# Handing a normalisation its tokens channel by row, with its squares summed by short matmuls

## The chip, the cores and the metric

The kernel runs on one core of a Trainium2 chip. The metric is the time of one execution on the device in microseconds, as a median over runs. A profiled execution gives, beside its own time, a trace of every engine: PE (TensorE, the matmuls), PEld (TensorE's weight loads), DVE (VectorE), ACT (ScalarE), POOL (GpSimd) and SP (SyncE, whose queue issues most transfers).

## The reference

Two layers over 256 latent tokens `x` and 256 context tokens `ctx`, each 2048 channels wide. The first layer normalises both, modulates them with a scale and a shift from a conditioning vector, and projects them with one wide matrix. Neighbourhood attention and a bidirectional state-space scan follow, an output projection and a residual; the second layer is a gated short convolution. What bears on the change is this:

```python
def rms_norm(x, g):
    xf = x.astype(jnp.float32)
    y = xf * lax.rsqrt(jnp.mean(xf * xf, axis=-1, keepdims=True) + EPS)
    return (y * g.astype(jnp.float32)).astype(x.dtype)
...
shift, scale, gate = adaln(c, ada_w[i], ada_b[i])
h = modulate(rms_norm(x, norm_g[i]), shift[:, None], scale[:, None])
...
shift_c, scale_c, gate_c = adaln(c_ctx, ada_w[i], ada_b[i])
hc = modulate(rms_norm(ctx, norm_g[i]), shift_c, scale_c)
...
p = h @ w_in
pc = hc @ w_in[:, base:]
```

So h = x * r * A + S, where r is one factor for a token (the norm), and A and S are one value for a channel, A = (1 + scale) * norm_g and S = shift, with a pair of A and S for x and another for ctx.

## The kernel before

**Channel blocks and segments.** The 2048 channels are the contraction of the first projection. They stand on the partitions in 16 blocks of 128 (`kb`), and the kernel takes them two by two in eight segments (`j`): for each segment the modulation values are made (`ada_gen`), then h for its two blocks, then the products with the segment's rows of the first K, V, Q and B columns are added to open sums. The columns of `hH` and `hL` are 512 tokens, numbered in four tiles t of 128: 0 and 1 are x, 2 and 3 are ctx.

**Split numbers.** A value is held as a high part rounded to fp32r and a low part, the difference. Each product is three matmuls: hH with the weight's high part, hL with the high part, hH with the low part. `hH` is written by ScalarE (L757), `hf`, the same in full fp32, by VectorE (L759), `hL` by VectorE as their difference (L763). A weight's high part is a cast on ScalarE (`split`, L420), its low part a subtraction on VectorE (`low_part`, L427). The very first weight (K of segment 0) is split in two halves (`split_half`, L440 and L443).

**The normalisation.** `x_load` brings a tile of 128 tokens, a token on each partition. `x_norm` squares and sums it in four pieces of 512 channels, ScalarE (L601) and VectorE (L603) in turn, sums the four (L607), makes the factor r with `rstd` (VectorE L571, then a power on POOL, L572), and multiplies the tile by r (L613, L615). `x_pair` then turns two channel blocks at a time with TensorE transposes of 128x128 (`turn`, L199), 64 in all, and copies them out of PSUM (L628 on ScalarE, L629 on VectorE) to `xnT`, channel on the partition. `x_gen` runs this for x, and for each tile of ctx alone in segment 0.

**The modulation.** For each segment and each of scale and shift, four quarters of 512 KB (`in_ada`) are multiplied with the conditioning vectors (`cpad`): four matmuls 128x256 to a quarter, on four groups of 32 columns. ScalarE copies the sum (`half`, L724), two transposes turn it, VectorE adds up the groups (L732) and adds the constants (L735 to L738).

**The order.** The program is written out once, at build, by a planner: `urgent`, `side` and `back` hold generators, each of which yields the engine and the operands that its next instruction needs; `pump` runs those whose operands are ready by the planner's own clock, and `force` runs on until a condition holds. Each engine then runs its instructions in that order and waits in order. Loads go out from a list (`loads`) in order as buffers come free; all are on SP's queue: the eight quarters of segment 0, its K, V and Q weights (512 KB each), ctx, the second parts of two small constant arrays (`small`, `const`), B's weight, segment 1's eight quarters, and so on. The matmul loop of segment 0 does K, V and Q for the tiles of x, then waits for tile 2 of ctx, does K and V for it, then tile 3, then B. In later segments K goes over all four tiles, then V, then Q (x only), then B. `part_gen` moves each K and V sum to SBUF (L787 copies, L789 adds).

## Time and profile before

| | |
|---|---|
| time, median of 3 runs | 1761.66 us (1761.09 to 1764.66) |
| profiled execution: its own time | 1760.31 us |
| profiled execution: span in the trace | 1758.5 us |
| PE busy | 1736.7 us (99%) |
| PEld busy | 1463.1 us (83%) |
| DVE busy | 1223.6 us (70%) |
| ACT busy | 773.4 us (44%) |
| POOL busy | 31.6 us (2%) |
| HBM traffic over the span | 215 GB/s |

Busy time is the time in which an engine has an instruction under way; the shares are of the span. The own time holds the span and 1.8 us around it. In the groups of the profile a row gives a line, an engine, an operation, output<-input by the program's names, shapes and count, then busy us and the mean ns of one, then the idle time just before and what ended it. A timeline row gives the start, the length, and the same description, with the idle time before it in brackets. The recorded matmuls of one fp32 product are two where those of an fp32r product are one.

### The profile page before, as it was taken

The page shows a single profiled execution, that of the slowest core. Times are in us where ns is not written, and L with a number is a line of the kernel's source. Part 1 is how long each engine was busy: PE and PEld are TensorE (multiplying, and loading weights), DVE is VectorE, ACT ScalarE, POOL GpSimd, SP SyncE. Part 2 cuts the span into 40 slices and gives each one's busy share as a digit, 9 for nine tenths or more (in the row PEclk, how much of TensorE's full clock was granted, in tenths as well). Part 3 has the DMA queues.
Part 4 walks back from the last instruction along what each step waited for, and adds up shares of the span by engine and source line. Part 5 has one row for each costly group of instructions (what it writes and reads, how often), then busy time and mean ns, then how long its engine had stood idle before and what let it go on. Part 6 is the DMA issues. An engine that isn't in the chain of part 4 may idle for free.

```text
span 1758.5 us, 25025 instructions
## 1 busy us (share of the span) xinstructions
PE 1736.7 (99%) x9451; PEld 1463.1 (83%) x9451; DVE 1223.6 (70%) x1978; ACT 773.4 (44%) x1330; POOL 31.6 (2%) x28
## 2 busy tenths in 40 slices
PE   6999999999999999999999999999999999999998
PEld 4777988889888889888888898888888888888887
DVE  5666887878685878686877787787668555555554
ACT  5333544445242436343435343564446444444442
POOL 0000100001000000000000000000000000000000
PEclk9999999999999999999999999999999999999999
DMA  9987644686756767656776557768767666666563
GB/s 362 342 307 258 209 143 138 183 246 191 234 165 195 219 205 227 210 175 210 220 213 193 166 185 255 246 221 284 274 222 228 195 188 192 192 191 188 190 208 121
DMA packets 202536, 377.66 MB, mean 215 GB/s; under 512 B 32384, under 2 KB 69040, under 8 KB 202416
## 3 DMA queue, kind: packets, MB, share of 16 engines
q1 hardware_dynamic: 195152, 369.49, 65.5%
q10 hardware_dynamic: 7264, 6.58, 1.1%
q8 instruction: 74, 1.21, 0.3%
q14 instruction: 46, 0.38, 0.1%
HBM read 370.62 MB, written 6.71 MB: 215 GB/s over the span
## 4 chain that ended last, share of the span: by engine, by line
PE 94%; DMA 2%; DVE 2%; issue 1%; ACT 0%; POOL 0%; SPq 0%; ACTq 0%; DVEq 0%; POOLq 0%
PE bank L195 91%; PE bank L199 3%; DMA tmp<-dram_csr 1%; DVE w L427 1%; DMA raw<-in_ada 0%; DMA tmp<-dram_exr 0%; DMA raw<-in_adaT 0%; DVE tmp L1235 0%; ACT w L420 0%; POOL statk L572 0%; DVE mix L1562 0%; SPq L583 0%; DVE raw L823 0%; DVE tmp L603 0%; DVE Vt L1012 0%
## 5 line engine op out<-in xcount | busy, mean ns | idle before, releaser
L420 ACT CAST w<-raw 128x1024 fp32r<-128x1024 f32 x343 | 359.5, 1049 | 530.4 <-PE bank L195 447.7
L427 DVE TENSOR_TENSOR w<-raw,w 128x1024 fp32r<-128x1024 f32 x343 | 416.6, 1217 | 231.4 <-ACT w L420 230.1
L195 PE MATMUL bank<-hH,w 128*128 128x256 f32 (+1 forms) x2064 | 488.0, 324 | 1.2 <-DVE w L427 1.1
L195 PE MATMUL bank<-w,hH 128*128 128x512 f32 x1280 | 407.4, 396 | 2.7 <-ACT hH L757 2.5
L195 PEld LDWEIGHTS bank<-hH,w 128*128 128x128 f32 x2064 | 344.7, 188 | 34.2 <-DVE w L427 2.1
L195 PE MATMUL bank<-hL,w 128*128 128x256 f32 (+1 forms) x1040 | 334.3, 321 | 0.0
L195 PEld LDWEIGHTS bank<-w,hH 128*128 128x128 f32 x1280 | 237.7, 189 | 54.4 <-issue 4.0
L195 PE MATMUL bank<-w,hL 128*128 128x512 f32 x640 | 249.9, 391 | 0.1
L195 PEld LDWEIGHTS bank<-hL,w 128*128 128x128 f32 x1040 | 196.3, 189 | 14.9
L195 PE MATMUL bank<-w,h 128*128 128x512 f32 x768 | 179.7, 390 | 0.0
L823 DVE CUSTOM_DVE_ANT_0 raw<-raw,csb 128x1024 f32<-128x1024 f32 x128 | 155.4, 1219 | 26.2 <-DMA raw<-in_adaT 24.0
L195 PEld LDWEIGHTS bank<-w,h 128*128 128x128 f32 x768 | 143.6, 188 | 29.6
L195 PEld LDWEIGHTS bank<-w,hL 128*128 128x128 f32 x640 | 120.5, 188 | 25.4 <-DVE hL L763 0.6
L195 PE MATMUL bank<-w,mix 128*128 128x512 f32 x588 | 138.3, 391 | 0.9 <-DVE w L427 0.9
L195 PEld LDWEIGHTS bank<-w,mix 128*128 128x128 f32 x588 | 109.5, 188 | 24.0 <-DVE w L427 1.3
L1235 DVE SCALAR_TENSOR_TENSOR tmp<-bank,cwh,tmp 128x508 f32<-128x508 f32 (+1 forms) x96 | 71.0, 744 | 1.8
L195 PE MATMUL bank<-KL,h 128*128 128x512 f32 x264 | 63.8, 389 | 0.0
L427 DVE TENSOR_TENSOR KL<-raw,KL 128x1024 fp32r<-128x1024 f32 x32 | 39.1, 1223 | 33.1 <-ACT KL L420 33.1
L427 DVE TENSOR_TENSOR wL<-raw,wH 128x1024 fp32r<-128x1024 f32 x31 | 37.9, 1224 | 33.5 <-ACT wH L420 33.4
L427 DVE TENSOR_TENSOR QL<-raw,QT 128x1024 fp32r<-128x1024 f32 x32 | 39.2, 1224 | 29.8 <-ACT QT L420 29.8
L195 PEld LDWEIGHTS bank<-KL,h 128*128 128x128 f32 x264 | 49.5, 188 | 10.2
L195 PE MATMUL bank<-QT,h 128*128 128x512 f32 x168 | 56.2, 391 | 0.0
(291 smaller groups left out, 1984.7 us busy)
## 6 DMA issues: line engine op xcount, KB each, us to landing
raw<-in_w_in SPq DMA_DIRECT2D x196, 512.0 KB, 3.9
raw<-in_adaT SPq DMA_DIRECT2D x128, 512.0 KB, 4.8
raw<-in_sc_in SPq DMA_DIRECT2D x128, 512.0 KB, 3.8
raw<-in_w_out SPq DMA_DIRECT2D x64, 512.0 KB, 5.0
raw<-in_ada SPq DMA_DIRECT2D x34, 512.0 KB, 6.9
raw<-in_sc_out SPq DMA_DIRECT2D x32, 512.0 KB, 4.1
PT<-in_ada SPq DMA_DIRECT2D x16, 512.0 KB, 6.9
raw<-in_w SPq DMA_DIRECT2D x16, 512.0 KB, 6.1
```

The costliest lines, as they stand in the source:

```text
L195: E(T.matmul(o, l, r, start=start, stop=stop, skip_group_check=True))
L199: E(T.transpose(o, i, ident if k == 128 else ident[:k, :k]))
L420: E(S.copy(H, v))
L427: E(V.tensor_tensor(out=Lo, in0=v, in1=H.bitcast(F32), op=ALU.subtract))
L823: E(V.tensor_tensor_reduce(out=raw, in0=raw, in1=csb, scale=1.0, scalar=0.0, op0=ALU.mult, op1=ALU.add, accum_out=gp[:, h, m:m + 1]))
L1235: E(V.scalar_tensor_tensor(out=do, in0=di, scalar=cwh[:, 32 * k + ch:32 * k + ch + 1], in1=do, op0=ALU.mult, op1=ALU.add))
```

## The change

The tokens come with the channels already on the partitions: beside `x`, which stays for the residual, the kernel gets `xt`, and in place of `cx` it gets `ct`, both turned by the host before the launch. The 64 transposes, their copies, the scaling of the tiles and `x_norm`, `x_pair` and `x_gen` go.

- `squares(c)` (c = 0 for x, 1 for ctx): eight squares 128x512 on ScalarE, each of two channel blocks for 256 tokens; six adds on VectorE bring the first seven into one; the sum over the partitions is by matmuls of 128x1 with a column of ones, four on the accumulated squares and four on the last, 16 in all for x and ctx. VectorE and POOL make r for 128 tokens by 2; two transposes of r, broadcast along a row, give r as a row on all partitions, and ScalarE copies it to `Rb`.
- In `ada_gen` hf is now x * A * Rb on VectorE, hH = hf + S on ScalarE behind it, and hL = (hf + S) - hH on VectorE, in 256 wide pieces for x and ctx (before, hL was one 512 wide from segment 1 on). The quarters of segment 0 are multiplied one by one as they come, no longer two by two.
- `c_load` brings all of ctx in six transfers (two of 512 KB, four of 256 KB) behind K and V of segment 0 and ahead of Q. Two pieces lie in the places of `QT` and `QL`, four in those of later hL blocks. The second parts of `small` and `const` come after the weights of segment 3.

```diff
 
     xrow = [st([128, D], "KT", name="x0")]
-    QT, Vt, gt = st([128, 4, 256], "QT", F32R), st([128, 4, 512], "Vt"), st([128, 4, 256], "gt")
+    cplace = [st([128, 1024], "QT", name="c0")]
+    Vt, gt = st([128, 4, 512], "Vt"), st([128, 4, 256], "gt")
     xrow.append(st([128, D], "KL", name="x1"))
-    QL = st([128, 4, 256], "QL", F32R)
+    cplace.append(st([128, 1024], "QL", name="c1"))
     sz, xtm, yi = st([128, 4, 256], "sz"), st([128, 2, 512], "xtm"), st([128, 4, 256], "yi")
     PT = [st([128, 4, 256], f"PT{k}") for k in range(2)]
 
@@ -527,11 +528,9 @@
             weight(w0, 3 * j + (CK, CV, CQ).index(c), 2, 0, 512)
 
     q_ada(0)
-    w_seg(0, CK, CV, CQ)
-    loads.append(lambda: x_load(2))
-    loads.append(lambda: x_load(3))
-    loads.append(lambda: E(DMA.dma_start(sm[:, NFIRST:], small[:, NFIRST:])))
-    loads.append(lambda: E(DMA.dma_start(cs_[:, CFIRST:], const[:, CFIRST:])))
+    w_seg(0, CK, CV)
+    loads.append(lambda: c_load())
+    w_seg(0, CQ)
     weight(w_in, 0, 2, COL_B, 256)
     q_ada(1)
     for j in range(1, 8):
@@ -540,6 +539,9 @@
             q_ada(j + 1)
         w_seg(j, CQ)
         weight(w_in, j * 256, 2, COL_B, 256)
+        if j == 3:
+            loads.append(lambda: E(DMA.dma_start(sm[:, NFIRST:], small[:, NFIRST:])))
+            loads.append(lambda: E(DMA.dma_start(cs_[:, CFIRST:], const[:, CFIRST:])))
     loads.append(later_loads)
...
-    XS = {}
     ssq = st([128, 16], "ssq")
-
-    def x_load(t):
-        src = x if t < 2 else cx
-        r0 = (t % 2) * 128
-        xt = xrow[t] if t < 2 else st([128, D], ("KT", "KL")[t % 2], name=f"x{t}")
-        for q in range(0, 4, 2):
-            E(DMA.dma_start(xt[:, q * 512:(q + 2) * 512], src[r0:r0 + 128, q * 512:(q + 2) * 512]))
-            XS[4 * t + q], XS[4 * t + q + 1] = (xt[:, p * 512:(p + 1) * 512] for p in (q, q + 1))
-
-    x_load(0)
-    x_load(1)
+    for k in range(2):
+        for h in range(2):
+            hs = slice(h * 1024, (h + 1) * 1024)
+            E(DMA.dma_start(xrow[k][:, hs], xt[k, :, hs]))
...
-    xnT = [st([128, 512], ("Bl", "Cl")[kb] if kb < 2 else f"hL{kb}", name=f"xm{kb}") for kb in range(KB)]
+    one, Rb, *lplace = [st([128, 512], ("Bl", "Cl")[kb] if kb < 2 else f"hL{kb}", name=f"p{kb}") for kb in range(KB)]
+    E(V.memset(one, 1.0))
+    cplace += lplace[10:]
+    xT = [[xrow[k // 8][:, (k % 8) * 256:(k % 8) * 256 + 256], None] for k in range(KB)]
     rx = st([128, 4], "rx")
 
-    def x_norm(t):
-        yield when(lambda: 4 * t + 3 in XS and (t < 2 or ("h", 0, 0) in got))
-        for q in range(4):
-            xt = XS[4 * t + q]
-            yield W_("ACT" if q % 2 == 0 else "DVE", xt)
-            jk = tmp()
-            if q % 2 == 0:
-                E(S.activation(jk, xt, AF.Square, accum_out=ssq[:, 4 * t + q:4 * t + q + 1]))
-            else:
-                E(V.tensor_tensor_reduce(out=jk, in0=xt, in1=xt, scale=1.0, scalar=0.0, op0=ALU.mult, op1=ALU.add,
-                                         accum_out=ssq[:, 4 * t + q:4 * t + q + 1]))
-            give(free_t, jk)
-        yield W_("DVE", ssq[:, 4 * t:4 * t + 4])
-        E(V.tensor_reduce(out=rx[:, t:t + 1], in_=ssq[:, 4 * t:4 * t + 4], axis=AX.X, op=ALU.add))
-        rstd(rx[:, t:t + 1], rx[:, t:t + 1], D, EPS, 1)
-        for q in range(4):
-            xt = XS[4 * t + q]
-            yield W_("DVE" if q % 2 else "ACT", rx[:, t:t + 1])
-            if q % 2 == 0:
-                E(S.mul(xt, xt, rx[:, t:t + 1]))
-            else:
-                E(V.tensor_scalar(out=xt, in0=xt, scalar1=rx[:, t:t + 1], scalar2=None, op0=ALU.mult))
-
-    def x_pair(k2, ts):
-
-        yield W_("PE", *[XS[4 * t + k2 // 2] for t in ts], nb=1)
-        ps = bank()
-        n = 128 * len(ts)
-        for k in range(2):
-            kb = 2 * k2 + k
-            for i, t in enumerate(ts):
-                turn(ps[:, k * n + i * 128:k * n + (i + 1) * 128], XS[4 * t + kb // 4][:, (kb % 4) * 128:(kb % 4) * 128 + 128])
+    def c_load():
+        n = 0
+        for p in cplace:
+            m = p.shape[1] // 256
+            E(DMA.dma_start(p, ct[:, n * 256:(n + m) * 256]))
+            for k in range(m):
+                xT[n + k][1] = p[:, k * 256:(k + 1) * 256]
+            n += m
+
+    def squares(c):
+
+        yield when(lambda: xT[15][c] is not None)
+        acc, ps = None, None
+        for k in range(0, KB, 2):
+            src = xrow[k // 8][:, (k % 8) * 256:(k % 8) * 256 + 512]
+            if c:
+                src = cplace[k // 4][:, (k % 4) * 256:(k % 4) * 256 + 512] if k < 8 else cplace[k // 2 - 2]
+            yield W_("ACT", src)
+            sq = tmp()
+            E(S.activation(sq, src, AF.Square))
+            if k < KB - 2:
+                if k == 0:
+                    acc = sq
+                    continue
+                yield W_("DVE", sq)
+                E(V.tensor_tensor(out=acc, in0=acc, in1=sq, op=ALU.add))
+                give(free_t, sq)
+                continue
+            for p in (acc, sq):
+                yield W_("PE", p, nb=0 if ps is not None else 1)
+                f = ps is None
+                if f:
+                    ps = bank()
+                for h in range(2):
+                    for t in range(2):
+                        mm(ps[:, t:t + 1], p[:, h * 256 + t * 128:h * 256 + (t + 1) * 128], one[:, :1], f and not (h or t), True)
+                give(free_t, p)
+        r = rx[:, 2 * c:2 * c + 2]
+        yield W_("DVE", ps)
+        E(V.tensor_scalar(out=r, in0=ps[:, :2], scalar1=1.0 / D, scalar2=EPS, op0=ALU.mult, op1=ALU.add))
+        E(G.tensor_tensor(out=r, in0=r, in1=mhalf[:, :2], op=ALU.pow))
+        yield W_("PE", r)
+        for t in range(2):
+            turn(ps[:, 256 + t * 128:256 + (t + 1) * 128], r[:, t:t + 1].to_broadcast([128, 128]))
         yield W_("ACT", ps)
-        o = slice(ts[0] * 128, ts[0] * 128 + n)
-        E(S.copy(xnT[2 * k2][:, o], ps[:, 0:n]))
-        E(V.tensor_copy(xnT[2 * k2 + 1][:, o], ps[:, n:2 * n]))
+        E(S.copy(Rb[:, c * 256:(c + 1) * 256], ps[:, 256:]))
         give(free_b, ps)
-        got.update(("xm", t, k2) for t in ts)
-
-    def x_gen(c):
-
-        ts = (2 * c, 2 * c + 1)
-        for t in ts:
-            yield from x_norm(t)
-            if c:
-                yield from x_pair(0, (t,))
-        for k2 in range(c, KB // 2):
-            yield from x_pair(k2, ts)
+        got.add(("r", c))
...
-                    w_ = 2 if j == 0 else 4
...
-            for ts in ((0, 1), (2,), (3,)) if j == 0 else ((0, 1, 2, 3),):
...
+            for cs in ((0,), (1,)) if j == 0 else ((0, 1),):
+                yield when(lambda: all(("r", c) in got for c in cs))
+                o = slice(256 * cs[0], 256 * cs[-1] + 256)
                 for kb in (2 * j, 2 * j + 1):
...
-                    yield W_("DVE", xnT[kb][:, o])
+                    yield W_("DVE", Rb[:, o])
                     hf = tmp()
                     if hH[kb] is None:
                         hH[kb] = st([128, 512], f"hH{kb}", F32R, name=f"hH{kb}")
-                    if ts == (0, 1):
+                    if cs == (0,):
                         split_half(kb)
-                    for k, ok_ in spans:
-                        E(S.activation(hH[kb][:, ok_], xnT[kb][:, ok_], AF.Identity, scale=A0[:, kb, k:k + 1],
-                                       bias=S0[:, kb, k:k + 1]))
-                        E(V.tensor_scalar(out=hf[:, ok_], in0=xnT[kb][:, ok_], scalar1=A0[:, kb, k:k + 1],
-                                          scalar2=S0[:, kb, k:k + 1], op0=ALU.mult, op1=ALU.add))
+                    for c in cs:
+                        oc = slice(256 * c, 256 * c + 256)
+                        E(V.scalar_tensor_tensor(out=hf[:, oc], in0=xT[kb][c], scalar=A0[:, kb, c:c + 1], in1=Rb[:, oc],
+                                                 op0=ALU.mult, op1=ALU.mult))
+                        E(S.activation(hH[kb][:, oc], hf[:, oc], AF.Identity, scale=1.0, bias=S0[:, kb, c:c + 1]))
                     if hL[kb] is None:
                         hL[kb] = st([128, 512], f"hL{kb}", F32R, name=f"hL{kb}")
-                    E(V.tensor_tensor(out=hL[kb][:, o], in0=hf[:, o], in1=hH[kb][:, o].bitcast(F32), op=ALU.subtract))
+                    for c in cs:
+                        oc = slice(256 * c, 256 * c + 256)
+                        E(V.scalar_tensor_tensor(out=hL[kb][:, oc], in0=hf[:, oc], scalar=S0[:, kb, c:c + 1],
+                                                 in1=hH[kb][:, oc].bitcast(F32), op0=ALU.add, op1=ALU.subtract))
                     give(free_t, hf)
-                    if ts == (0, 1):
+                    if cs == (0,):
                         halfsplit.pop()()
-                if ts == (0, 1):
+                if cs == (0,):
                     hold[0] = False
                     split()
                     split()
-                got.update(("h", j, t) for t in ts)
+                got.update(("h", j, t) for c in cs for t in (2 * c, 2 * c + 1))
...
-    spawn(urgent, x_gen(0), 1)
+    spawn(urgent, squares(0), 2)
     spawn(urgent, ada_gen(), 2, 1)
-    spawn(urgent, x_gen(1), 1)
+    spawn(urgent, squares(1), 2)
...
+    QT, QL = st([128, 4, 256], "QT", F32R), st([128, 4, 256], "QL", F32R)
...
-        'x': f('x')[0], 'cx': f('ctx')[0], 'ada0': ada0, 'w0': w0, 'adaT': adaT, 'w_in': f('na_ssd_w_in')[0],
+        'x': f('x')[0],
+        'xt': f('x')[0].T.reshape(2, 8, 128, 256).transpose(0, 2, 1, 3).reshape(2, 128, 2048),
+        'ct': f('ctx')[0].T.reshape(16, 128, 256).transpose(1, 0, 2).reshape(128, 4096),
+        'ada0': ada0, 'w0': w0, 'adaT': adaT, 'w_in': f('na_ssd_w_in')[0],
```

More of the change, by code (lines that the diff above doesn't have):

```diff
@@ L141, with kernel @@
 @with_exitstack
-def kernel(ctx: ExitStack, tc, x, cx, ada0, w0, adaT, w_in, w_out, sc_in, sc_out, rpb, small, const,
+def kernel(ctx: ExitStack, tc, x, xt, ct, ada0, w0, adaT, w_in, w_out, sc_in, sc_out, rpb, small, const,
                        strict, rows, out):
@@ L709, in ada_gen @@
                     key = ("ada", j, part, q)
-                    w_ = 2 if j == 0 else 4
+                    w_ = 1 if j == 0 else 4
                     if q % w_ == 0:
@@ L739, in ada_gen @@
                 give(free_b, ps)
-            for ts in ((0, 1), (2,), (3,)) if j == 0 else ((0, 1, 2, 3),):
-                yield when(lambda: all(("xm", t, j) in got for t in ts))
-                spans = [(k, slice(max(256 * k, 128 * ts[0]), min(256 * k + 256, 128 * ts[-1] + 128)))
-                         for k in range(2) if {2 * k, 2 * k + 1} & set(ts)]
-                o = slice(128 * ts[0], 128 * ts[-1] + 128)
+            for cs in ((0,), (1,)) if j == 0 else ((0, 1),):
+                yield when(lambda: all(("r", c) in got for c in cs))
+                o = slice(256 * cs[0], 256 * cs[-1] + 256)
                 for kb in (2 * j, 2 * j + 1):
@@ L1989 @@
     force(lambda: not urgent, (urgent,))
-_INS = ['x', 'cx', 'ada0', 'w0', 'adaT', 'w_in', 'w_out', 'sc_in', 'sc_out', 'rpb', 'small', 'const', 'strict', 'rows']
+_INS = ['x', 'xt', 'ct', 'ada0', 'w0', 'adaT', 'w_in', 'w_out', 'sc_in', 'sc_out', 'rpb', 'small', 'const', 'strict', 'rows']
 def kernel(**inputs):
```

## The prediction

> **What bounds the kernel now.** I read first the page's chain of work that ended last, then the busy time by stretches, then PE's timeline up to 56 us, then ScalarE's and VectorE's there.
>
> ```profile
> PE 94%; DMA 2%; DVE 2%; issue 1%; ACT 0%; POOL 0%; SPq 0%; ACTq 0%; DVEq 0%; POOLq 0%
> ...
> 21.00:24.50 3.50, 1.89 (x12) 0.96 (x8) 1.92 (x6) 2.70 (x6) 0.00 (x0) 1.00 1.03 406
> 24.50:28.00 3.50, 3.50 (x10) 2.73 (x10) 3.40 (x6) 3.08 (x7) 0.00 (x0) 0.52 1.02 405
> 28.00:33.50 5.50, 5.50 (x26) 4.50 (x25) 2.68 (x10) 3.32 (x6) 0.55 (x1) 0.99 1.05 399
> 33.50:45.00 11.50, 9.75 (x99) 6.19 (x98) 6.69 (x23) 6.90 (x19) 1.06 (x3) 1.00 0.84 326
> 55.00:165.00 110.00, 109.78 (x747) 80.62 (x746) 65.49 (x124) 34.28 (x54) 0.00 (x0) 1.00 0.84 305
> ```
>
> The columns of the stretches are the stretch, its length, busy PE, PEld, DVE, ACT, POOL, then the granted TensorE clock, the DMA share and GB/s. From 55 to 165 us PE rests 0.22 us in all, and the chain is 94% PE: once the first projections run, whatever PE has lost stays lost to the end. VectorE is busy 65 of 110 us there, ScalarE 34, so small work added or removed on them is hidden. The change's instructions all lie ahead of that, so its worth is the moment at which PE reaches the common work, the first group of the second segment.
>
> ```profile
> 10.82 2.28 PE L195 MATMUL bank<-raw,cpad 128*32 128x256 f32 x16 [10.82 <-DMA raw<-in_ada]
> 13.03 4.36 PE L199 MATMUL bank<-const,x 128*128 128x128 f32 x32
> 23.35 0.74 PE L195 MATMUL bank<-w,hH 128*128 128x512 f32 x2 [1.11 <-ACT hH L757]
> 33.40 0.38 PE L199 MATMUL bank<-const,x 128*128 128x128 f32 x2
> 35.13 0.50 PE L195 MATMUL bank<-w,hH 128*128 128x512 f32 x1 [1.36 <-ACT hH L757]
> 38.82 0.87 PE L199 MATMUL bank<-const,x 128*128 128x128 f32 x6 [0.31 <-ACT x L613]
> 43.61 1.05 PE L195 MATMUL bank<-raw,cpad 128*32 128x256 f32 x16
> 44.59 1.09 PE L199 MATMUL bank<-const,x 128*128 128x128 f32 x8
> 45.74 1.04 PE L199 MATMUL bank<-const,x 128*128 128x128 f32 x8
> 54.30 0.50 PE L195 MATMUL bank<-w,hH 128*128 128x512 f32 x1
> 55.23 0.48 PE L195 MATMUL bank<-w,hH 128*128 128x512 f32 x1
> ```
>
> Before the first projection (23.35) PE is held by the modulation weights (the quarters of ada0), which arrive by DMA: the first at 10.82. Then x's half of K, V, Q keeps it busy to 33.4. There the context's two tiles are late: it waits 1.36 at 35.13 and 0.31 at 38.82. The modulation of segment 1 ends with the row at 43.61, near 44.5; call that P0. The second block of segment 1's K starts at 55.23, P0+10.7.
>
> **Step 1, the start.** The 32 transposes at 13.03 lie under the quarters' arrival, and so will the eight short sums that replace them; PE may begin some 1 us earlier than 23.35, since ada0's shift is summed quarter by quarter. But nothing comes of it: PE only runs sooner into the context, which is later, as follows.
>
> **Step 2, the context.** Loads were K, V, Q, context, constants; now K, V, four context loads, Q. By the stretches 406 GB/s moves 512 KB in 1.29 us.
>
> ```profile
> 27.23 0.63 ACT L601 ACTIVATE tmp<-x 128x512 f32<-128x512 f32 x1 [0.42 <-DMA x<-in_cx]
> L420 ACT CAST w<-raw 128x1024 fp32r<-128x1024 f32 x4 | 4.0, 1046 | 0.0
> L427 DVE TENSOR_TENSOR w<-raw,w 128x1024 fp32r<-128x1024 f32 x4 | 4.7, 1220 | 0.0
> L601 ACT ACTIVATE tmp<-x 128x512 f32<-128x512 f32 x8 | 5.0, 622 | 0.9 <-DMA x<-in_x 0.4 <-DMA x<-in_cx 0.4
> L443 DVE TENSOR_TENSOR w<-yi,w 128x512 fp32r<-128x512 f32 x2 | 1.4, 684 | 0.0
> L195 PE MATMUL bank<-const,half 128*128 128x1 f32 x4 | 0.5, 230 | 0.0
> L1462 POOL TENSOR_TENSOR r<-r,const 128x2 f32<-128x2 f32 x8 | 6.9, 858 | 335.9 <-DVE r L1460 294.6 <-DVE s L1066 41.3
> L724 ACT COPY half<-bank 128x256 f32<-128x256 f32 x5 | 1.9, 372 | 7.5 <-PE bank L195 7.5
> L763 DVE TENSOR_TENSOR hL<-tmp,hH 128x256 fp32r<-128x256 f32 x2 | 0.9, 426 | 0.4 <-ACT hH L757 0.3
> L763 DVE TENSOR_TENSOR hL<-tmp,hH 128x512 fp32r<-128x512 f32 x2 | 1.4, 692 | 0.5 <-ACT hH L757 0.4
> L757 ACT ACTIVATE hH<-xm,S,A 128x256 fp32r<-128x256 f32 x6 | 3.4, 602 | 1.4 <-DVE S L738 1.4
> L199 PE MATMUL bank<-const,x 128*128 128x128 f32 x64 | 8.8, 290 | 0.3 <-ACT x L613 0.3
> ```
>
> When does Q land? The context's second load landed at 27.23, fifth from K; Q is now about as many bytes after it as two loads: 29.8. Counted instead from 10.82 at 1.29 each (seven more quarters, K, V, four context, Q: 14 steps) it is 28.9. I take 29.2, with both as ends. In the changed kernel's instruction order ScalarE has Q's cast ahead of all eight context squares, and VectorE has Q's low part (L427) ahead of the six adds. So: cast 1.05, low part 1.22, then six adds that depend on each other, at 0.68 and some 0.06 between, 4.4 in all (the squares, near 0.55 apart, keep ahead of them), with hops 6.9. The accumulated squares are ready at 29.2+6.9 = 36.1; call it tA. PE runs out of x's work near 33.3, so it waits nearly 3 us where it waited 1.4.
>
> From tA on everything is one chain: 8 short sums, 16 recorded matmuls at 0.5/4 at most, 2.0; the factor's affine step 0.2; its power on POOL, 0.86 in the mean of the like row, taken 0.8; two transposes 0.4; copy of the row 0.37; hf on VectorE 0.43 (nearest row: the 128x256 hL, 0.426); hH on ScalarE 0.60; hops 0.3: 5.1. Segment 1's scale quarters run under it (nearest rows: 16 in 1.05 at most, four of them some 1.8). Then hL and the second block's hf and hH, each waiting for the other engine, and PE's queue behind the wait is in order: the transposes of the scale's half stand behind the second hH, at tA+6.9. Behind them two groups of three 512-wide matmuls for K and six for V, plus the shift's four quarters: 12 x 0.23 + 1.8 + 0.2 = 4.7. (0.23 is the stretch from 28.00: 5.50 us over 24 such, its other two rows aside.) So P0 = 36.1 + 6.9 + 4.7 = 47.7, against 44.5: **+3.2**, from 2.9 (Q at 28.9) to 3.8.
>
> **Step 3, the first groups of segment 1.** Of the 64 transposes 32 lie after 23.35; at about 0.11 each (16 from 44.59 to 46.78, less the overlap of the records and a pair for the half between) that is 3.5 us, and for the 16 after P0 1.7. What is late next?
>
> ```profile
> 49.25 1.11 ACT L757 ACTIVATE hH<-xm,S,A 128x256 fp32r<-128x256 f32 x2
> 50.25 2.00 ACT L420 CAST w<-raw 128x1024 fp32r<-128x1024 f32 x2
> 51.33 2.36 DVE L427 TENSOR_TENSOR w<-raw,w 128x1024 fp32r<-128x1024 f32 x2
> ```
>
> Segment 1's K low part began at 51.33, P0+6.8, in time for 54.30, because the transposes still occupied PE. In the new order VectorE has it behind the last hL of block 3, which waits for that block's two hH, and ScalarE has these behind the casts of K and V (before, the hH at 49.25 came ahead of the casts at 50.25). Worked forward from P0: shift sum on VectorE at 1.6; both hH of block 2 at 3.2; copy of gt, casts and copy of Vt to 6.2 (0.6 + 2.0 + 0.6, less overlap); two hH to 7.0; second hL, then K's low part at 8.6. PE has only a transpose pair, nine 512-wide matmuls and B's twelve, and arrives at 5.5: **a new stall of 3.1 us**. Two of that block's three products don't need the low part; the third, and segment 2's scale (1.8), end at P0+10.65. Before it was 10.7. The transposes' 1.7 us and segment 2's shorter queue go into the stall: **0**. Were K's low part in time it would be -3.1; were the hops longer by 0.1 each, +0.5.
>
> **Step 4, the clock.** In 21.00 to 24.50 PE was busy 1.89 of 3.50, and the next 3.5 us had a granted clock of 0.52; in the stretch with 9.75 of 11.5 busy it stayed 1.00. A stall of 3.1 us leaves a window emptier than 1.89 of 3.5, so I expect 0.52 for about 3.4 us after it, on work that PE bounds: 3.4 x 0.48 = **+1.6**, from 0 (no such window) to 1.7. The wait before tA should do the same to the short sums and the transposes, but there PE isn't the bound for most of the window: 0 to 1.2, taken 0. The Trainium skill, TensorE: Matmul & The Clock Gate, Part 1 (the HAM clock gate), says that half clock comes after at least one idle window of about 3.4 us; a 3.1 us stall cannot fill one, so by it this term is 0 and the sum is +3.2. This trace speaks against it: a window with 1.89 us of work was enough.
>
> **Edits at nothing.** The constants (small, const) go from near 29 us to behind segment 3's weights; DMA is at 0.84 of its time from 55 to 165 us and PE never waits there, so a 0.4 MB transfer (1 us) is hidden; if that cover were gone, 1 us. hL in two 256-wide pieces instead of one 512 costs VectorE 2x0.43 against 0.69, and hf's other form next to nothing, against 44 us of VectorE's idle time there. Uncovered, the 0.17 would come once per block, 2 us over twelve blocks; but from segment 2 on no low part is ordered behind a late hH.
>
> **Sum.** +3.2 + 0 + 1.6 = +4.8 against the profiled execution's own 1760.31 (span 1758.5): 1765.1. The median of the runs shown, 1761.66, is 1.35 above that execution; a shift adds alike, so the forecast is 1766.5.
>
> **The rivals.** A measurement of this kernel can tell about 0.2%, 3.5 us, from no change: faster is under 1758.1, slower over 1765.2.
>
> *The context comes in time.* If Q's cast and low part don't delay the squares (tA by 33.4) and segment 1's K low part comes by P0+5.5, the 3.5 us of transposes, the 1.7 us of waits and the early start's 1.0 count, and the sums and two transposes put back 2.4: -3.8, 1757.9. For it: PE's waits at 35.13 and 38.82 belong to what is removed. Against: Q's place behind four context loads, and the order on ScalarE. Both conditions must hold: 0.10.
>
> *No half clock.* As forecast, but PE keeps its clock: +3.2, 1764.9; with Q at 28.9, 1764.6. A stall that falls astride two windows would leave neither emptier than 1.89 of 3.5 and leads here too: 0.28 for within 0.2%. The Trainium skill's rule above would lead here.
>
> *Two slow windows.* Q at 29.8, and the window after the wait before tA lengthens the sums: 3.8 + 1.6 + 1.2 = +6.6, 1768.3. It decides if the sums start later than 36.5: 0.17, inside slower.
>
> *The change doesn't do what it says*: the 64 transposes are out of the new instruction order and from about PE's 790th instruction both orders agree, so I give it 0.
>
> **The numbers.** Forecast 0.45 and two slow windows 0.17 make slower 0.62; within 0.2% 0.28; faster 0.10. The range runs from 1758.5, just above the faster case, to 1769.5, the two windows and 1.2 for the scatter of the runs shown (1761.09 to 1764.66); the likeliest case alone has 1764.6 to 1768.5.
>
> **What would show it.** In the profile after: Q's cast ahead of the eight squares and the first short sum of the context near 36; a PE wait before it of 2 to 3 us; the first context projection near 41; the shift's quarters ending near 47.7; a PE wait of about 3 us on segment 1's K low part; a stretch at about 0.5 of the clock behind it. It is wrong if PE shows no such wait, or if the waits shrink and the end comes before 1758.

## The result and the profile after

The changed kernel took 1769.62 us (median of 13 runs, 1765.86 to 1773.35); beside it on the same chip the kernel before took 1764.40 (13 runs, 1760.56 to 1769.22). The ratio is 1.0031, interval 1.0018 to 1.0044: slower by 5.2 us in medians, where +4.8 was forecast. The predicted 1766.5 was 3.1 too low, because the base under it, the median of only three runs, was 2.7 too low, and the time lies 0.1 above the end of the range, 1769.5. One execution each of two later versions, of 6222 and 2936 us, is left out of every figure below.

The profiled execution after took 1773.35, the slowest of its 13, and that of before 1760.31, below all 13 of its kernel here. So the two traces overstate the difference, and a second trace of the changed kernel is read beside the first.

First the chain of work that ended last, after:

```profile
PE 92%; DMA 3%; DVE 2%; ACT 1%; issue 1%; SPq 0%; POOL 0%; ACTq 0%; DVEq 0%; POOLq 0%
```

PE is still the bound: 92% where it was 94%. Then the busy time by stretches, after (stretch, length, busy PE, PEld, DVE, ACT, POOL, granted clock, DMA share, GB/s):

```profile
24.50:28.00 3.50, 3.50 (x9) 2.06 (x10) 2.86 (x6) 1.91 (x3) 0.00 (x0) 0.70 1.05 396
33.50:45.00 11.50, 8.44 (x59) 5.15 (x58) 5.48 (x11) 5.73 (x12) 1.22 (x3) 0.76 0.63 248
55.00:165.00 110.00, 107.21 (x722) 76.85 (x722) 68.85 (x130) 32.24 (x55) 0.00 (x0) 0.98 0.81 296
...
39.40:42.80 3.40, 2.56 (x22) 1.28 (x26) 1.03 (x4) 0.88 (x2) 1.22 (x3) 0.52 0.04 12
42.80:46.20 3.40, 3.40 (x22) 1.78 (x14) 1.00 (x3) 0.88 (x2) 0.00 (x0) 0.50 0.71 257
56.00:59.50 3.50, 0.81 (x5) 0.35 (x3) 2.08 (x4) 1.78 (x4) 0.00 (x0) 1.00 1.00 369
59.50:63.00 3.50, 3.50 (x33) 1.63 (x33) 1.07 (x1) 0.00 (x0) 0.00 (x0) 0.57 0.73 255
```

Two things stand out against before. From 55 to 165 us PE now rests 2.8 us instead of 0.2. And the clock, which before was low only once ahead of 165 us (24.5 to 28, where it is low after, too), is also at half from 39.4 to 46.2 and again from 59.5 to 63. PE's timeline, after, says where (start, length, line, operation, and in brackets the idle time ahead of it and what ended it):

```profile
11.40 3.57 PE L196 MATMUL bank<-p,tmp 128*128 128x1 f32 x16 [11.40 <-DVE tmp L616]
24.50 0.73 PE L196 MATMUL bank<-w,hH 128*128 128x512 f32 x2 [1.36 <-ACT hH L755]
37.26 1.95 PE L196 MATMUL bank<-p,tmp 128*128 128x1 f32 x16 [2.02 <-DVE tmp L616]
40.24 0.69 PE L200 MATMUL bank<-const,rx 128*128 128x128 f32 x2 [1.04 <-POOL rx L631]
40.86 1.94 PE L196 MATMUL bank<-raw,cpad 128*32 128x256 f32 x16
44.43 0.80 PE L196 MATMUL bank<-w,hH 128*128 128x512 f32 x1
50.08 1.05 PE L196 MATMUL bank<-raw,cpad 128*32 128x256 f32 x16
59.49 0.50 PE L196 MATMUL bank<-w,hH 128*128 128x512 f32 x1 [2.69 <-DVE w L428]
63.47 0.50 PE L196 MATMUL bank<-w,hH 128*128 128x512 f32 x1
```

The context's short sums wait 2.02 us for VectorE's adds (37.26); its first product comes at 44.43, the shift's quarters end near 51.05 (the prediction's P0, 44.5 before), and PE then waits 2.69 us for segment 1's K low part. The second block of that K starts at 63.47; before, at 55.23. ScalarE and VectorE show the two queues behind these waits:

```profile
30.31 1.05 ACT L421 CAST w<-raw 128x1024 fp32r<-128x1024 f32 x1 [2.80 <-DMA raw<-in_w]
31.27 2.19 ACT L610 ACTIVATE tmp<-c 128x512 f32<-128x512 f32 x4
54.49 2.01 ACT L421 CAST w<-raw 128x1024 fp32r<-128x1024 f32 x2
56.87 0.92 ACT L755 ACTIVATE hH<-tmp,S 128x256 fp32r<-128x256 f32 x2
```

```profile
31.39 1.23 DVE L428 TENSOR_TENSOR w<-raw,w 128x1024 fp32r<-128x1024 f32 x1 [2.57 <-ACT w L421]
32.54 4.67 DVE L616 TENSOR_TENSOR tmp<-tmp,tmp 128x512 f32<-128x512 f32 x6
57.42 0.88 DVE L760 SCALAR_TENSOR_TENSOR hL<-tmp,S,hH 128x256 fp32r<-128x256 f32 x2 [1.99 <-ACT hH L755]
58.22 2.35 DVE L428 TENSOR_TENSOR w<-raw,w 128x1024 fp32r<-128x1024 f32 x2
```

Q's cast waits for Q's landing (30.3) ahead of the squares, and Q's low part stands ahead of the adds. Later K's low part (58.22) stands behind two hL, which wait for two hH, which stand behind the casts. Both are as forecast.

A second profile of the changed kernel (1769.38 us) separates what recurs from the chance of one execution:

> The changed kernel once more, unchanged, for a second trace of it. Theory A: PE's two waits (2.0 ahead of the context's sums, 2.7 at segment 1's K low part) are there again within 0.3 us, the short sums start near 37 and the first context product near 42 to 44.5, by whether half clock falls on the chain. Rival C (the waits are an accident of that execution): one of them is gone or under half as long.

Its timeline of PE:

```profile
35.84 2.07 PE L196 MATMUL bank<-p,tmp 128*128 128x1 f32 x16 [1.43 <-DVE tmp L616]
43.15 0.80 PE L196 MATMUL bank<-w,hH 128*128 128x512 f32 x1
48.41 1.05 PE L196 MATMUL bank<-raw,cpad 128*32 128x256 f32 x16
57.81 0.66 PE L196 MATMUL bank<-w,hH 128*128 128x512 f32 x1 [2.69 <-DVE w L428]
61.72 0.50 PE L196 MATMUL bank<-w,hH 128*128 128x512 f32 x1
```

and its stretches around the two waits:

```profile
37.00:40.50 3.50, 2.46 (x22) 1.59 (x25) 0.76 (x3) 0.37 (x1) 1.22 (x3) 0.57 0.58 233
58.00:61.50 3.50, 3.50 (x33) 1.39 (x32) 0.90 (x1) 0.00 (x0) 0.00 (x0) 0.51 0.77 273
```

Both waits recur, and half clock behind each, so they belong to the kernel; the first wait is 0.6 us shorter, more than the 0.3 expected. Here Q landed at 28.9 instead of 30.3, and the sums came 1.4 us sooner.

### The profile page after: what moved, and what is told of

Its sections match the earlier page's. It is cut to its first block, busy times and chain, and to the rows that moved or that the text cites. A ratio compares the mean times of both kernels' runs of the same rounds, so it can differ in the third digit from the quotient of the medians.

```text
span 1771.6 us, 24894 instructions
## 1 busy us (share of the span) xinstructions
PE 1743.2 (98%) x9423; PEld 1464.4 (83%) x9423; DVE 1220.5 (69%) x1954; ACT 764.9 (43%) x1305; POOL 31.8 (2%) x26
## 4 chain that ended last, share of the span: by engine, by line
PE 92%; DMA 3%; DVE 2%; ACT 1%; issue 1%; SPq 0%; POOL 0%; ACTq 0%; DVEq 0%; POOLq 0%
PE bank L196 89%; PE bank L200 3%; DMA tmp<-dram_csr 1%; DVE w L428 1%; DMA raw<-in_w 1%; DMA x<-in_xt 0%; DMA raw<-in_w_in 0%; ACT w L421 0%; DMA tmp<-dram_exr 0%; ACT tmp L610 0%; DVE tmp L1234 0%; DMA raw<-in_adaT 0%; DMA bias<-dram_rpbs 0%; DVE raw L821 0%; ACT tmp L1399 0%
## 5 line engine op out<-in xcount | busy, mean ns | idle before, releaser
L428 DVE TENSOR_TENSOR KL<-raw,KL 128x1024 fp32r<-128x1024 f32 x32 | 39.2, 1225 | 32.7 <-ACT KL L421 32.5
L428 DVE TENSOR_TENSOR wL<-raw,wH 128x1024 fp32r<-128x1024 f32 x31 | 38.0, 1225 | 33.5 <-ACT wH L421 33.4
L428 DVE TENSOR_TENSOR QL<-raw,QT 128x1024 fp32r<-128x1024 f32 x32 | 39.2, 1225 | 29.8 <-ACT QT L421 29.8
```

Source lines behind the costliest of these rows:

```text
L428: E(V.tensor_tensor(out=Lo, in0=v, in1=H.bitcast(F32), op=ALU.subtract))
```

## How much of it is the clock

Each run's record gives its span and mean granted clock. Span times (1 - clock) is the time lost to a low clock, as far as PE bounds; what remains is called the rest. Means over the runs: the changed kernel 1769.8 = 6.1 lost + 1763.7 rest. The kernel before, in the three groups of runs that stood beside the experiments (25, 33 and 23 runs), lost 2.0, 2.2 and 1.5 on a rest of 1762.5, 1761.5 and 1761.6. (The clock is recorded to 0.001, so one run's split is uncertain by some 0.9 us; the means less so. A low clock in the last microseconds, in which PE no longer works, counts as lost too: 1.1 us of it in a second trace of before. And the first 14 to 24 us have no clock on record, as the last section shows.) So the clock gives +3.9 to +4.6 and the waits, less the transposes saved, +1.1 to +2.2. That is an accounting, not yet a cause; the experiments test it.

## The experiments

Ratios are to the kernel before in runs on the same chip; runs of one group share those of before (medians 1765.17, 1764.04 and 1762.92).

**Segment 1's K low part without its queue.** In segment 1, VectorE takes K's low part ahead of the second block's hf and hL:

```diff
+                    if j == 1 and kb == 3 and lows:
+                        low_part()
```

> One edit to the changed kernel: segment 1's K low part is put on VectorE ahead of block 3's hf and hL (it stood behind them). Theory A: PE's wait of 2.69 us there goes nearly whole, and with it the window at half clock behind it (1.7 us): 3 to 4.4 us below the changed kernel, 1.0005 to 1.0015 of the kernel before. Theory B: the wait was slack that the late start had made; another wait takes its place within the segment, and the ratio stays near 1.003.

Ratio 1.0008 (0.9996 to 1.0019), median 1766.18: as expected, and level with before. PE's timeline:

```profile
40.98 1.94 PE L196 MATMUL bank<-raw,cpad 128*32 128x256 f32 x16
57.97 0.50 PE L196 MATMUL bank<-w,hH 128*128 128x512 f32 x1 [0.50 <-ACT hH L757]
```

and the stretch behind the place of the stall:

```profile
58.00:61.50 3.50, 3.48 (x38) 1.95 (x38) 2.57 (x4) 0.32 (x1) 0.00 (x0) 1.00 0.97 358
```

The 2.69 us wait is down to 0.50, and the half clock behind it is gone. K's second block starts at 57.97, ahead of segment 2's quarters; in the changed kernel it stood behind them, so these rows can't be compared. PE's order is the same again from 86.15 in the trace after and 83.86 here. Up to that point it takes 32.7 us from the end of the shift's quarters (51.16) and not 35.1, so 2.4 us are gained in this trace. The half clock in the context's chain stays: 16 quarter matmuls take 1.94 at 40.98, where full clock gives 1.05. Its rest is 1762.4, that of before; what it still costs is clock (4.3 lost against 2.0). So the stall and the half clock behind it are most of the 5.2 us by the runs: 3.2 by the means (1766.6 against 1769.8), 4 by the ratios, where the one trace shows 2.4.

**PE kept busy in both waits.** Results of the added matmuls aren't read; 8 stand ahead of the context's short sums, 11 ahead of the product that waits for segment 1's K low part:

```diff
+                if f and c:
+                    for _ in range(8):
+                        T.matmul(ps, hH[0][:, :128], w3[0][0][:, 0], ...)
...
+            if (j, key, t, k) == (1, "K", 0, 0):
+                spare_b = take(free_b)
+                for _ in range(11):
+                    T.matmul(spare_b, hH[0][:, :128], HLo[0][:, k], ...)
```

> The changed kernel with 19 matmuls 128x512 added whose results nobody reads: 8 ahead of the context's short sums, 11 ahead of the product that waits for segment 1's K low part. They fill PE's two waits (2.0 and 2.7 us) and leave the waits' causes as they are. Theory A with the clock (step 4: a window emptier than 1.89 of 3.5 us is followed by 3.4 us at half clock, and there PE bounds): the granted clock stays near 1.00 from 36 to 46 us and behind 56 us, 3 to 4 us are gained, 1.0005 to 1.0015 of the kernel before. Rival C (half clock has another cause, such as the short and the 32-column matmuls, or costs nothing because PE is not the bound there): the same time as the changed kernel or up to 0.5 us more, 1.003.

Ratio 1.0015 (1.0003 to 1.0027), at the edge of what the clock theory had: with work added the mean is 1767.2, 2.6 under the change without it, where 3 to 4 were expected. The two intervals overlap; the trace carries the reading. PE's timeline, and the stretches:

```profile
35.14 1.97 PE L626 MATMUL bank<-w,hH 128*128 128x512 f32 x8
37.33 1.95 PE L196 MATMUL bank<-p,tmp 128*128 128x1 f32 x16 [0.21 <-DVE tmp L616]
40.67 1.07 PE L196 MATMUL bank<-raw,cpad 128*32 128x256 f32 x16
42.53 0.50 PE L196 MATMUL bank<-w,hH 128*128 128x512 f32 x1
57.47 0.49 PE L196 MATMUL bank<-w,hH 128*128 128x512 f32 x1 [0.21 <-DVE w L428]
59.75 0.50 PE L196 MATMUL bank<-w,hH 128*128 128x512 f32 x1
```

```profile
33.50:45.00 11.50, 9.73 (x74) 6.95 (x73) 5.90 (x14) 5.67 (x13) 1.21 (x3) 1.00 0.68 271
55.00:165.00 110.00, 109.59 (x740) 79.68 (x740) 70.09 (x132) 31.36 (x53) 0.00 (x0) 1.00 0.83 300
```

The sums start where they did in the first trace after (37.33 against 37.26), so the squares were no earlier; but the clock stays at 1.00, and the first context product follows 5.2 us behind them instead of 7.2. From the end of the shift's quarters (49.03) to K's second block it is 10.7 us instead of 12.4. Lost time falls from 6.1 to 3.2, the rest stays (1764.0). That a wait of PE can cost twice, once as a wait and once as half clock behind it, is shown by this run.

**Q's load before the context's.** Q's load follows K's and V's at once, so that it doesn't land behind the 2 MB of the context:

```diff
-    w_seg(0, CK, CV)
+    w_seg(0, CK, CV, CQ)
...
-    w_seg(0, CQ)
```

> One edit to the changed kernel: Q's load goes ahead of the context's loads, so ScalarE and VectorE split Q first and the context's squares are made as their pieces come. Theory A (the forecast's step 2: the squares stand behind Q's cast and low part, 6.9 us after a late Q): the accumulated squares are ready before PE has done x's work at 34.9, the first context product comes near 40 and not at 44.4; a stall of some 1.4 us at segment 1's K stays, since its casts now stand ahead of block 2's hH. 4 to 6 us below the changed kernel, 0.9995 to 1.0010 of the kernel before. Theory B (the start: 16 recorded short sums of x, 3.57 us, stand ahead of the first quarter, so x's work starts at 24.50 and not 23.35, and the rest follows): that is untouched here, so at most 1 us is gained and the ratio stays near 1.003.

Ratio 1.0043 (1.0026 to 1.0060): missed; Theory B's 1.003 lies within the interval. The local step came out as expected (first context product near 40), and it was given back at once:

```profile
40.20 0.79 PE L196 MATMUL bank<-w,hH 128*128 128x512 f32 x1 [1.52 <-ACT hH L754]
43.38 1.94 PE L196 MATMUL bank<-raw,cpad 128*32 128x256 f32 x16
```

The scale's quarters, which filled PE under the chain (40.86 after), now come at 43.38, behind the first product. PE waits 1.52 there and 1.76 in segment 1 (57.76), and the quarters still run at half clock. Lost time is 7.8. It isn't a clean undo of Q's place, because the order of PE's work moved with it.

**Q's load before the context's, and K's cast and low part early**, right behind segment 0's B:

```diff
-    w_seg(0, CK, CV)
+    w_seg(0, CK, CV, CQ)
...
-    w_seg(0, CQ)
...
+                if j == 1 and part == 1:
+                    yield when(lambda: pos["split"] > 4)
+                    hold[0] = True
...
+            hold[0] = True
...
+            if pos["split"] == 4:
+                split()
+            while lows:
+                low_part()
```

> Both edits: Q's load ahead of the context's, and segment 1's K cast and low part right behind B's, ahead of the shift's copy. Theory A: first context product near 40, no wait above 0.5 us at segment 1's K; 6 to 9 us below the changed kernel, 0.998 to 0.9998 of the kernel before, since the 32 transposes behind 23.35 are now a gain. Theory B: x still starts at 24.50, and the kernel stays at 1.001 to 1.003.

1.0034 (1.0021 to 1.0047): missed. The waits moved again (1.23 at 35.54, 1.52 at 40.77, 1.44 at 73.35).

**The context's squares before Q's cast.** ScalarE holds Q's cast back until the eight squares are issued, and the sums stand between x's V and Q:

```diff
-            w3 = [use(k) for k in range(3)]
+            w3 = [use(k) for k in range(2)]
+            hold[0] = True
+            force(lambda: ("q", 1) in got, (urgent,))
+            w3.append(use(2))
...
+            force(lambda: ("s", 1) in got, (urgent,))
+            hold[0] = False
```

> The loads as in the changed kernel; written out in another order: the eight context squares and their adds stand ahead of Q's cast and low part on ScalarE and VectorE, and the context's short sums stand on PE between x's V and x's Q, so that the factor is made while PE works on Q. Theory A (the chain from the last square to the first context product, 7.2 us in the changed kernel, has nothing beside it on PE): accumulated squares near 32.6 (37.2 in the changed kernel), first context product near 38 (44.4), and no wait there above 1 us. A stall of about 2 us is left at segment 1's first block, where both hH stand behind the casts of K and V: 1.0000 to 1.0015 of the kernel before. Theory B (x's late start and what it moves): 1.003.

1.0038 (1.0025 to 1.0051): missed. Sums earlier, but new waits of 2.0 at 33.5, 2.4 at 58.4 and two smaller ones; 6.2 lost, rest 1764.7.

**The same with K's cast and low part early**, by the lines of the edit before that bear on K:

> The same, and segment 1's K cast and low part right behind B's, ahead of the shift's copy and of both hH. Theory A: the stall at segment 1's first block falls under 0.8 us; the kernel comes to the level of the kernel before or under it, 0.9985 to 1.0002. Theory B: 1.002 to 1.003.

1.0038 (1.0024 to 1.0051): missed. Here the clock loss does fall, to 4.4, but the rest rises to 1766.1. PE's timeline:

```profile
32.70 1.95 PE L196 MATMUL bank<-p,tmp 128*128 128x1 f32 x16 [1.44 <-DVE tmp L616]
```

The sums come 4.6 us sooner than after, and the gain is spent in small waits, 0.77 at 54.32 and others after it, to 136 us. The order of work is planned as the kernel is built, and the edit changed it: PE's is the same again only from 170.6 us on (172.8 after). So neither run tells what an early context alone would bring; that stays open.

**The start.** x's squares are folded on VectorE, so that two short sums stand behind the first quarter instead of eight ahead of it, alone and together with the edit before (context's squares first, K early):

```diff
-            if k < KB - 2:
+            if k < KB - 2 or not c:
...
+                if k == KB - 2:
+                    E(V.tensor_tensor(out=acc[:, :256], in0=acc[:, :256], in1=acc[:, 256:], op=ALU.add))
...
+                    for t in range(2):
+                        mm(ps[:, t:t + 1], acc[:, t * 128:(t + 1) * 128], one[:, :1], not t, True)
```

> The changed kernel with x's squares folded on VectorE alone (2 short matmuls for x in place of 8), all else as it is. Theory A: x's work starts some 1 us sooner, PE only waits longer for the context: no gain, 1.002 to 1.0035. Theory B (x's late start is what costs): 1 to 2.5 us below the changed kernel, 1.0015 to 1.002.

> The same, and x's squares summed further on VectorE (the last square too, then one half on the other), so that x needs 2 short matmuls and not 8. They are 4 recorded ones, some 0.5 to 0.9 us, behind the first quarter. PE starts on x's work near 23.4 and not 24.5. Theory A: 0 to 1 us below the kernel without it, since the context still comes at the same time, 0.998 to 1.0000. Theory B: the whole loss goes here, 1.2 us and more below the one without it.

Alone 1.0037 (1.0022 to 1.0052), near what Theory A had; with the others 1.0044 (1.0029 to 1.0059), missed by both theories. PE's timeline of the first:

```profile
10.83 1.08 PE L196 MATMUL bank<-raw,cpad 128*32 128x256 f32 x8 [10.83 <-DMA raw<-in_ada]
24.08 0.73 PE L196 MATMUL bank<-w,hH 128*128 128x512 f32 x2 [1.36 <-ACT hH L762]
35.75 1.95 PE L196 MATMUL bank<-p,tmp 128*128 128x1 f32 x16 [1.50 <-DVE tmp L616]
56.58 0.49 PE L196 MATMUL bank<-w,hH 128*128 128x512 f32 x1 [2.65 <-DVE w L428]
57.01 1.07 PE L196 MATMUL bank<-PT,cpad 128*32 128x256 f32 x16
```

The first quarter runs at 10.83 again, but x's products start only 0.4 of the 1.15 us sooner, so this is a weak test. What speaks against the theory that the late start costs time is the wait ahead of the context's sums, which is longer than 1.15: 2.02 after, 1.50 here. It takes up whatever the start loses.

This trace shows something else. The stall of 2.65 us is there, but the quarters behind it run at full speed: 16 in 1.07 (57.01), where they took 1.91 after. So half clock doesn't follow every such wait.

**Everything at once.** The edit that takes K's low part ahead of hf, with 18 unread matmuls: 6 small ones ahead of x's first product, 8 ahead of the context's sums, 4 behind them:

```diff
+            for _ in range(6):
+                T.matmul(psk[0][:, :128], ident, ident, ...)
...
+                    for _ in range(8):
+                        T.matmul(ps, hH[0][:, :128], w3[0][0][:, 0], ...)
...
+        for _ in range(4 if c else 0):
+            T.matmul(ps[:, 256:], hH[0][:, :128], w3[0][0][:, 0, :256], ...)
...
+                    if j == 1 and kb == 3 and lows:
+                        low_part()
```

> The changed kernel with segment 1's K low part ahead of block 3's hf and hL (as in e2_k1_early), and with 18 matmuls added whose results nobody reads: 6 of 128x128 ahead of x's first product, 8 of 128x512 ahead of the context's short sums, 4 of 128x256 behind them. The clock is what most of the loss is (Theory A with the clock): mean granted clock 0.998 to 0.999, and 3 to 5 us below the changed kernel beyond doubt, 0.998 to 1.000 of the kernel before. Rival C (filling does not matter where the wait itself is gone): no better than the kernel with the early low part alone, 1.0008.

1.0033 (1.0021 to 1.0046): missed. The clock loss came out as expected (3.0), the rest rose to 1765.2. The timeline shows part of the price:

```profile
26.34 0.73 PE L196 MATMUL bank<-w,hH 128*128 128x512 f32 x2
37.66 1.84 PE L196 MATMUL bank<-p,tmp 128*128 128x1 f32 x16
```

x's first product is 1.8 us later than in the trace after, but not by the fillers ahead of it: it follows the modulation's last product by 1.36 us, as after, and that came later because the quarters ahead of it still ran at half speed (8 records in 1.08 at 22.86, where 8 take 0.61 at 21.48 after). The context's sums start without any wait, 1.3 us behind VectorE's last add (36.39), so there the fillers held PE when it could have gone on. And in this trace they didn't keep the clock:

```profile
38.50:42.00 3.50, 3.20 (x31) 2.32 (x35) 0.83 (x3) 0.44 (x2) 1.22 (x3) 0.90 0.14 52
42.00:45.50 3.50, 3.50 (x30) 1.83 (x22) 1.37 (x3) 1.32 (x3) 0.00 (x0) 0.61 0.76 256
```

The clock is at half from 41.3 to 44.7 although PE is recorded busy for 3.11 of the 3.41 us before that, 1.6 of them in short sums. Whether short sums count as little for the clock isn't tested. How much of the 2.8 us by which the rest stands over that of the K edit alone comes from the fillers isn't settled.

**The kernel before, again and kept warm.** A second profile of it, and the kernel with 6 unread matmuls ahead of x's first product and 4 ahead of context tile 2:

```diff
+        for _ in range(4 if (j, key, t) == (0, "K", 2) else 0):
+            T.matmul(ps, hH[0][:, :128], HLo[0][:, 0], ...)
...
+            for _ in range(6):
+                T.matmul(psk[0][:, :128], ident, ident, ...)
```

> The kernel before once more, unchanged, for a second trace of it. Theory A: waits as in the first trace (1.11 at 23.35, 1.36 at 35.13), one window at half clock near 24 to 28, and a mean granted clock of 0.998 to 1.000 where the changed kernel has 0.995 to 0.997.

> The kernel before with 10 matmuls added whose results nobody reads: 6 of 128x128 ahead of x's first product (its wait of 1.11 us), 4 of 128x512 ahead of the first product of the context's first tile (its wait of 1.36 us). Theory A with the clock: the window at half clock behind 24.5 us (3.4 us at 0.52) goes in most executions: 0.5 to 1.7 us below the kernel before, 0.9990 to 0.9997. Rival C: 1.0000 or slightly above.

The second profile took 1762.02, as expected. With fillers the ratio is 0.9995 (0.9982 to 1.0008). The stretch that had 0.52 of the clock before, in the kernel with fillers:

```profile
24.50:28.00 3.50, 3.50 (x15) 2.25 (x14) 3.40 (x6) 3.31 (x7) 0.00 (x0) 1.00 1.02 403
```

The half clock is gone, and lost time falls from 1.5 to 0.8, but a gain of 0.7 us is under what can be told. No version that was run is clearly faster than the kernel before.

## Where the prediction held and where it failed

Two numbers in the sum failed: the half clock in the context's chain, which was taken as 0 and cost some 2 us (step 4), and the base, 1761.66, which was 2.7 too low. The mechanisms of steps 2 and 3 came as forecast.

**Step 1, the start: wrong in sign, worth nothing.** x began 1.15 us later (24.50), not 1 earlier: eight short sums, 16 records, took 3.57 us at 11.40, ahead of the first quarter, and the work behind them ran at half speed up to 19.0 us, before only to 14.4 (last section). That nothing comes of it held: the wait ahead of the context's sums is longer than what the start lost.

**Step 2, the context: right in mechanism and hops.** The order of casts, squares, low part and adds is as forecast. From Q's landing to the accumulated squares 6.9 us were forecast, and both traces after show it (30.3 to 37.2, 28.9 to 35.8). Q's landing, with bounds 28.9 and 29.8, was at 28.9 in one trace and 30.3 in the other. The chain from there to the first product, 5.1 forecast, was 5.2 with PE kept warm and 7.2 to 7.3 without. In the second trace P0 was at 49.4: 47.4 without the 2.0 us of clock, at an early Q, as forecast for that.

**Step 3, segment 1's K low part: right in mechanism.** A stall of 3.1 forecast, 2.69 in both. From P0 to the second block 12.4 (51.05 to 63.47) and 12.3, which is the 10.7 of before and the half clock of step 4. So at that point the transposes' 1.7 us did go into the stall. Taking the stall away didn't bring them back: over the same work, up to the point from which PE's order is the same, the version with the early low part takes 32.7 us from P0, and the kernel before, with 16 transposes more, 32.4 (33.1, less 0.7 for three products that stand ahead of P0 in the other). Smaller waits took their place.

**Step 4, the clock: the term that was mis-sized.** The +1.6 behind the stall came in both traces of the changed kernel, though not in that with x folded, where a stall of 2.65 us is followed by full speed. The clock on record changes in steps of 3.41 us, and there the stall lies across two of them, as the prediction's rival without half clock had it: PE is busy 1.81 us of one (52.12 to 55.53) and 2.37 of the next. The one in the context's chain was "taken 0", with the reason that PE isn't the bound there. It cost some 2 us in each trace, since the scale's quarters, counted as hidden under the chain, doubled (32 records from 40.86 to 44.43) and became what ended last ahead of the first product. In the first trace the sum is 1.1 of late Q, 2.0 of clock in the chain, 3.2 and 1.7 as forecast: 8.0 of the 8.2 us by which K's second block moved (55.23 to 63.47).

**The rival that came.** Two slow windows, given 0.17, is what the traces show: half clock behind both waits, though in the first it lengthened the quarters, and not the sums (1.95) as the rival had it. It was said to decide if the sums start later than 36.5; they start at 37.26 in one trace and 35.84 in the other, and it came in both, so that point was set too late. The no-half-clock rival fell for the two traces. The Trainium skill, TensorE: Matmul & The Clock Gate, Part 1 (the HAM clock gate), led there, with half clock only after an idle window of about 3.4 us. The changed kernel's traces don't agree: waits of 2.02 and 1.04 us with the short sums between them, and a single one of 2.69, were followed by 0.50 to 0.57 of the clock, as were the shorter ones of the second trace; the measurement decides. But the busy time of the stretch before, by which the prediction went, doesn't decide either: 1.81 of 3.41 us left the clock full with x folded, and 3.11 of 3.41, short sums among them, were followed by half clock with everything at once. What does is open.

**The base, and why +4.8 was nearly right.** The traces moved by 8.2 and 6.5 us at K's second block, the medians by 5.2. Over many runs the accounting gives +1.1 to +2.2 of waits and +3.9 to +4.6 of clock, against +3.2 and +1.6 forecast, so the sum came near by luck, with one term too large and one too small. By the same split the two profiles of before are 1.8 lost + 1758.6 and 3.5 + 1758.5: their rest is some 3 to 4 us under the mean rest of its runs, while the changed kernel's (1764.5 and 1764.1) is at its own. Where an average run of before spends those 3 us the traces don't show, though the waits named next vary by as much; it stays open, and with it the size of the waits' term. The low base is a matter of three runs.

**Later in the kernel** both kernels have a wait that varies from run to run, near 1122 us before and 1132 after. Before and after, in the first traces:

```profile
1122.46 6.90 PE L195 MATMUL bank<-w,mix 128*128 128x512 f32 x29 [0.91 <-DVE w L427]
```

```profile
1134.01 8.50 PE L196 MATMUL bank<-w,mix 128*128 128x512 f32 x29 [1.50 <-DVE w L428]
```

With the half clock behind it (8.50 for the same 29 matmuls instead of 6.90) it explains 1.6 us of the first trace after, and the same wait was 0.44 us, with 6.90, in the second. With a wait for ScalarE just ahead of it, it comes to 2.1 us in the second trace of before and 4.0 with x folded, so it belongs to the scatter and not to the change. Waits near 680 and 697 us, 0.8 us in one trace after and 1.6 in the other, are in none of the three traces of before, but also missing in several versions of the changed kernel; whether the change makes them more likely isn't shown.

## What to carry to other kernels

On an engine that bounds a kernel, price a wait of some 2 us twice: as the wait, and as the half clock that can, but need not, follow it, above all if work counted as hidden runs in that stretch. A removed operation is worth what the next one in line leaves: here 1.7 of the 3.5 us of transposes went into a stall on a low part whose place in VectorE's queue nobody had needed to care for while the transposes covered it. And a base of three runs is itself a term of the sum, with its own scatter of 2 to 3 us.

## What the runs showed of the hardware

Short sums are dear for their size: 16 records of 128x1 took 1.95 us at full clock (37.26) and 3.57 near the start (11.40), about 0.12 and 0.22 each, against 0.23 for a 512-wide matmul. There the granted clock of the stretch, after, reads 1.00:

```profile
11.00:14.50 3.50, 3.10 (x15) 3.10 (x15) 0.35 (x1) 0.00 (x0) 0.00 (x0) 1.00 1.02 414
```

and yet other work runs at half speed there too: with x folded, 8 quarter records took 1.08 at 10.83, where 16 take 1.05 later. The 1.00 isn't a measurement: the trace's record of the clock begins only at 19.0 us after (14.4 before, 21.4 with x folded, 24.2 with everything at once), and a stretch without record reads as 1.00. Half speed lasts up to about that point in each: after, 8 quarter records take 0.64 from 20.17 on. So the start is at half clock, as far as the speed of the work shows it, and the sums' two times are one at full and one at half speed. Filling a wait with matmuls that nobody reads kept the clock at 1.00 in one version (33.50 to 45.00, 0.76 without), at no price that can be told where they end before the data comes, and didn't in another (0.61 from 42.00 to 45.50).
